# Three low parts taken from SBUF and one bank copied by ScalarE in the first gate/up unit

## The chip, the cores and the metric

The kernel runs on one core of a Trainium2 chip. The metric is the device time of one execution in microseconds (us), the median of the runs. The core has five engines with queues of their own: PE (TensorE, with its weight loads shown as PEld), DVE (VectorE), ACT (ScalarE), POOL (GpSimd) and SP, which here only issues transfers. Each engine takes its instructions in order, so an instruction that waits holds up everything behind it on that engine.

## The reference

One layer of a decoder on 512 tokens of width 2048, in float32: a combined input projection, two groups of attention heads, an output projection, a SwiGLU block and a last RMSNorm. The change touches the first matrix product of the SwiGLU block.

```python
D_MODEL = 2048; SEQ = 512
D_FF = -(-8 * D_MODEL // (3 * 256)) * 256          # 5632
...
x = x + mixed @ w_out[l]
h = rmsnorm(x, ln_ffn[l])
gate, up = jnp.split(h @ w_gate_up[l], 2, axis=-1)
x = x + (jax.nn.silu(gate) * up) @ w_down[l]
```

## The kernel before

**Rounded and low parts.** PE multiplies in a rounded float32 form (fp32r). To keep precision, every operand is split in two: a rounded part, "hi", which an ACT copy writes, and a low part, "lo" = value minus rounded part, which a DVE subtraction writes. Weights are stationary: tile `whi` holds their hi, `wlo` their lo (two buffers each). The other side lies in tiles whose 512 columns are 256 of hi and 256 of lo; a product takes `whi` against all 512 columns and `wlo` against the 256 of hi.

**Units and products.** `h @ w_gate_up` is done in 44 units (`Unit(j)`), each of 128 gate and 128 up columns. A unit cuts both sides into 2 by 2 blocks and makes seven block products in place of eight, in the order `PR` = 1, 7, 2, 5, 4, 6, 3. A product has a first half (four blocks of 128 rows, s = 0) and a second half (s = 1). In the first unit each half runs four matmuls with `whi` and then four with `wlo`. Products 1, 2 and 6 go to a PSUM bank named `m`, the others to one named `o`; product 6 is added onto the bank of product 1, 4 onto that of 7, 3 onto that of 5, so the earlier value is copied out first: `get_p1` and `get_p7` copy the banks of products 1 and 7 to slices of the SBUF tile `w4` (`w` in the profile).

**Weights of a product.** They are either loaded (`raw`, `rawx`) or a difference of loaded blocks that POOL makes (`sum`, tiles `t`; for products 7 and 5 of the first unit they share one tile, `t7`). `to_hp` lets ACT write a second rounded copy to a PSUM tile `hp`; `to_hi` lets ACT write the same values to `whi` in SBUF; `to_lo` lets DVE subtract `hp` from the weights. A `whi` buffer is free once the second half of the product two before has finished with it on PE.

**Other side.** It is made once and used by all 44 units. `form(p, s)` makes it for product p: "+" builds the sum or difference of blocks of `xh` (the scaled, transposed activations; `xh` again in the profile), "h" is the ACT copy and "l" the DVE subtraction. The tiles are named `hcs`, `hco`, `hca` and `hct`. The first halves (s = 0) and the second halves of products 1 and 7 are ready before the first unit; the second halves of 2, 5, 4, 6 and 3 are made while the first unit runs. Product 3's sum (`xh<-xh`) is POOL's, the others are DVE's.

**Order.** All of this stretch is in the order in which the code is written: `pV`, `pA`, `pG`, `pT` and `dma` record for DVE, ACT, POOL, PE and SP and keep that order (one helper, L118). `start_unit(n)` writes what follows product n of the first unit. Also there, on POOL, are five steps on tiles of 128x4 that make the scale of the second RMSNorm (`rv`, `rt`, `rq`), then a transfer (`q`), then product 3's sum.

**Buffers.** `e8` tiles (128 x 2048 floats) have three buffers in pool `side`: the tile `w4` of the first unit takes the buffer that `t7` had, so whatever writes `w4` first waits until every reader of `t7` is done; the last of these is the `to_lo` of product 5.

Of the kernel before, what the change touches and what calls it, by code (L numbers as in the profile page):

```python
# [12 lines left out]
AF = mybir.ActivationFunctionType  # L13
ALU = mybir.AluOpType
# [23 lines left out]
def tile_hymba(ctx: ExitStack, tc: tile.TileContext, x, ln_mix, w_in, sb_norm, swa_norm,  # L38
# [63 lines left out]
    def f(ap):  # L102
        return ap.bitcast(F32)
# [16 lines left out]
    pV, pA, pG, pT = Pinned(V), Pinned(A), Pinned(G), Pinned(nc.tensor)  # L120
# [792 lines left out]
    def h2_split(c, between=None):  # L913
        eV, eT = (pV, pT) if c == 3 else (V, nc.tensor)
        xh[c] = (o8.tile([P, 4, 512], F32, tag="o8", name="xh") if c < 2 else e8("xh"))
        if c == 3:
            two = zs[1].tile([P, 2, 512], F32, tag="hp", name="xt", bufs=2)
            pbs = [po(), po(), two[:, 0, :], two[:, 1, :]]
        else:
            pbs = [pz() for k4 in range(4)]  # L920
        for k4 in range(4):
            for t in range(NT):
                eT.transpose(out=pbs[k4][:, t * P:(t + 1) * P], in_=x2[c][:, t, k4 * P:(k4 + 1) * P], identity=ident)
        if between:
            between()
        for k4 in range(4):
            kt = c * 4 + k4
            eV.scalar_tensor_tensor(out=xh[c][:, k4, :], in0=pbs[k4], scalar=gcol[:, 16 + kt:17 + kt], in1=rs1["b"],
                                    op0=ALU.mult, op1=ALU.mult)
# [10 lines left out]
    def form(p, s, parts="+hl"):  # L940


        eV, eA = (pV, pA) if s and p not in "17" else (V, A)
        xa, xb = xh[2 * s], xh[2 * s + 1]
        a11, a21 = xa[:, :, 0:256], xa[:, :, 256:512]
        if p not in "17":
            a12, a22 = xb[:, :, 0:256], xb[:, :, 256:512]
        if "+" in parts:
            if p == "7":
                src = e8("s3")[:, 0:2, :].rearrange("p u (a b) -> p (u a) b", a=2)  # L950
                V.tensor_tensor(out=src, in0=a11, in1=a21, op=ALU.subtract)
            elif p == "5":
                src = a21
                eV.tensor_tensor(out=src, in0=a21, in1=a22, op=ALU.add)
            elif p == "6":
                src = a11
                eV.tensor_tensor(out=src, in0=a21, in1=a11, op=ALU.subtract)
            elif p == "3":
                src = a12
                (pG if s else G).tensor_tensor(out=src, in0=a12, in1=a11, op=ALU.subtract)  # L960
            else:
                src = {"1": lambda: a11, "2": lambda: a12, "4": lambda: a22}[p]()
            fsrc[p, s] = src
        src = fsrc[p, s]
        if "h" in parts:
            hc[p, s] = form_tile(p, s)
            eA.activation(out=hc[p, s][:, :, 0:256], in_=src, func=AF.Copy)
        if "l" in parts:
            hl = hc[p, s]
            eV.tensor_tensor(out=hl[:, :, 256:512], in0=src, in1=f(hl)[:, :, 0:256], op=ALU.subtract)  # L970
# [70 lines left out]
    def squares(c, ts):  # L1041
        for t in ts:
            pA.activation(out=junk, in_=x2[c][:, t, :], func=AF.Square, accum_out=ss2[:, t, c:c + 1])
# [4 lines left out]
    class Weights:  # L1048
# [15 lines left out]
        def to_lo(self, p):  # L1064
            src = self.src(p)
            self.lo[p] = wp.tile(list(src.shape), F32R, tag="wlo", name="wlo", bufs=2)
            pV.tensor_tensor(out=self.lo[p], in0=src, in1=f(self.hp[p]), op=ALU.subtract)

    class Unit(Weights):

# [73 lines left out]
            pA.activation(out=self.p1, in_=self.bank["1"], func=AF.Copy)  # L1144

        def get_p7(self):
            pV.tensor_copy(out=self.p7, in_=self.bank["7"])

        def get_c11(self):
            self.c = e8("c4")  # L1150
# [200 lines left out]
    def of(n, what):  # L1351

        if n < NP:
            getattr(units[n // 7], what)(PR[n % 7])
        elif n < NS:
            c, i = divmod(n - NP, 2)
            if what == "product":
                plain.product(c, i)
            elif i == 0:
                getattr(plain, what)(c)  # L1360
        elif n < NS + ND:
            getattr(passes[(n - NS) // 14], what)((PD[(n - NS) % 14 // 2], (n - NS) % 2))
# [30 lines left out]

    def between():
        squares(3, (3,))
        of(2, "to_hp")

    h2_split(3, between)
    units[0].product("1", ((1,),))
    upper.close()  # L1400
# [111 lines left out]
    def start_unit(n):  # L1512
        u = units[0]
        if n == 0:
            of(2, "to_hi")
            of(2, "to_lo")
            form("5", 1, "+")
            form("2", 1)
        elif n == 1:
            of(3, "to_hp")  # L1520
            of(3, "to_hi")
            of(3, "to_lo")
            u.get_w4()
            u.get_p7()
            form("5", 1, "hl")
        elif n == 2:
            of(4, "to_hp")
            of(4, "to_lo")
            form("4", 1)
            of(4, "to_hi")  # L1530
            u.get_p1()
        elif n == 3:
            form("6", 1, "+")
            of(5, "to_hp")
            of(5, "to_lo")
            of(5, "to_hi")
            form("6", 1, "hl")
            form("3", 1, "+")
        elif n == 4:
            of(6, "to_hp")  # L1540
            u.get_p75()
            of(6, "to_lo")
            form("3", 1, "hl")
            of(6, "to_hi")
        else:
            of(7, "to_hp")

    for n in range(NS + ND):
        if n > 1:
            run(n, "load")  # L1550
        run(n, "sum")
        if n > 5:
            of(n + 1, "to_hi")
            of(n + 1, "to_lo")
            of(n + 2, "to_hp")
        if n > 6:
            of(n, "product")
        elif n:
            units[0].product(PR[n], ((0,), (1,)))
        if n < 6:  # L1560
            start_unit(n)
        run(n, "take")
        run(n, "late")
# [95 lines left out]
```

## Time and profile before

| | |
|---|---|
| median of 3 runs | 2020.99 us (2020.88 to 2021.22) |
| profiled execution | 2021.5 us, of which its instructions span 2019.4 us |
| granted TensorE clock | 0.999 |
| PE busy | 2004.3 us, 99% of the span, 10412 matmuls |
| DVE, ACT busy | 1456.5 us, 1456.0 us (72% each) |
| POOL busy | 1030.2 us (51%) |
| the first unit's stretch | 722.7 to 746.2 us after the span's start |

In a row of the timeline, the columns are start in us from the span's start, duration in us, engine, line, operation, tile written <- tiles read, shape, count, and in brackets idle time of the engine just before it with what ended it. A duration runs to the end of the write; the next instruction of the engine can start some 0.1 us earlier, so steps on one engine are counted by the distance of their starts.

### The profile page before, as it was taken

What the parts mean: (1) busy time and instruction counts of PE and PEld (TensorE: products, weight loads), DVE (VectorE), ACT (ScalarE), POOL (GpSimd) and SP (SyncE); (2) the same over time, 40 slices, a digit from 0 to 9 for tenths busy, and PEclk for the clock granted to TensorE, in tenths of its full rate; (3) what the DMA queues carried; (4) which work ended last, traced back from release to release, by engine and by line L of the source; (5) the groups of instructions that cost most, each with busy time, mean ns of one, the idle gap of its engine ahead of it and who ended that gap; (6) DMA issues with size and microseconds to landing.
All of it is one profiled execution on the core that took longest, in us unless ns stands there. A gap on an engine that the chain in (4) does not pass through costs nothing. (4 is left out here: it accounts for less than half of the span.)

```text
span 2019.4 us, 29249 instructions
## 1 busy us (share of the span) xinstructions
PE 2004.3 (99%) x10412; PEld 1708.3 (85%) x10412; DVE 1456.5 (72%) x1968; ACT 1456.0 (72%) x2009; POOL 1030.2 (51%) x562
## 2 busy tenths in 40 slices
PE   9999999999999999999999999999999999999998
PEld 8888888898888888888888888888888888888886
DVE  4358888778963777777777777777777967767767
ACT  5347777657842478777777777777777688788787
POOL 0014444300100066766667666676666678878883
PEclk9999999999999999999999999999999999999999
DMA  5322222222343354453544535444354733533523
GB/s 188 94 84 73 63 63 73 64 77 71 105 146 115 117 160 121 115 141 100 136 116 120 138 100 139 113 123 133 103 141 109 288 130 107 178 132 105 175 86 115
DMA packets 286369, 240.23 MB, mean 119 GB/s; under 512 B 11024, under 2 KB 237392, under 8 KB 283792
## 3 DMA queue, kind: packets, MB, share of 16 engines
q1 hardware_dynamic: 285552, 235.71, 39.4%
q8 instruction: 82, 1.34, 0.3%
q0 software_dynamic: 288, 1.32, 0.2%
q10 hardware_dynamic: 384, 1.34, 0.2%
q14 instruction: 63, 0.52, 0.1%
HBM read 218.40 MB, written 19.92 MB: 118 GB/s over the span
## 5 line engine op out<-in xcount | busy, mean ns | idle before, releaser
L118 POOL TENSOR_TENSOR t<-raw,t 128x1024 f32<-128x1024 f32 x107 | 272.2, 2544 | 277.5 <-ACT hp L118 263.7
L118 DVE TENSOR_TENSOR wlo<-t,hp 128x1024 fp32r<-128x1024 f32 x235 | 286.4, 1219 | 172.3 <-PE o L118 108.1
L118 ACT ACTIVATE whi<-t 128x1024 fp32r<-128x1024 f32 x235 | 249.2, 1061 | 123.3 <-PE o L118 75.2
L118 PE MATMUL o<-hca,whi 128*128 128x512 f32 x880 | 307.5, 391 | 0.0
L118 POOL TENSOR_TENSOR t<-raw,raw 128x1024 f32<-128x1024 f32 x106 | 276.0, 2608 | 15.6 <-issue 10.9
L118 DVE TENSOR_TENSOR wlo<-raw,hp 128x1024 fp32r<-128x1024 f32 x175 | 213.5, 1220 | 79.9 <-issue 49.7
L118 ACT ACTIVATE whi<-raw 128x1024 fp32r<-128x1024 f32 (+1 forms) x177 | 187.1, 1057 | 99.9 <-PE m L118 72.1
L118 PE MATMUL o<-hca,wlo 128*128 128x256 f32 x880 | 244.0, 280 | 0.0
L118 ACT ACTIVATE hp<-t 128x1024 fp32r<-128x1024 f32 x235 | 237.0, 1008 | 0.3 <-DVE wlo L118 0.3
L220 DVE TENSOR_TENSOR wlo<-raw,whi 128x1024 fp32r<-128x1024 f32 x103 | 128.1, 1243 | 136.0 <-ACT whi L219 133.4
L219 ACT ACTIVATE whi<-raw 128x1024 fp32r<-128x1024 f32 x103 | 108.8, 1056 | 154.3 <-PE o L360 76.8
L118 PEld LDWEIGHTS o<-hca,whi 128*128 128x128 f32 x880 | 164.2, 187 | 35.8
L118 PE MATMUL m<-hca,whi 128*128 128x512 f32 x528 | 186.3, 392 | 1.1 <-DVE hca L118 1.1
L118 ACT ACTIVATE hp<-raw 128x1024 fp32r<-128x1024 f32 x179 | 180.7, 1010 | 3.2 <-DMA raw<-in_w_down_dram 2.3
L118 PEld LDWEIGHTS o<-hca,wlo 128*128 128x128 f32 x880 | 165.6, 189 | 0.4
L390 PE MATMUL m<-hhi,whi 128*128 128x512 f32 x384 | 156.3, 407 | 0.0
L391 PE MATMUL m<-hlo,whi 128*128 128x512 f32 x384 | 150.5, 392 | 0.0
L392 PE MATMUL m<-hhi,wlo 128*128 128x512 f32 x384 | 150.4, 392 | 0.0
L118 PE MATMUL o<-whi,dca 128*128 128x512 f32 x592 | 147.0, 389 | 1.5 <-DVE x2r L118 1.5
L118 PE MATMUL m<-whi,dca 128*128 128x512 f32 x592 | 146.9, 389 | 0.0
L118 PE MATMUL m<-hca,wlo 128*128 128x256 f32 x528 | 146.3, 280 | 0.0
L118 PEld LDWEIGHTS o<-whi,dca 128*128 128x128 f32 x592 | 111.1, 188 | 24.8 <-DVE x2r L118 1.9
(351 smaller groups left out, 5146.3 us busy)
## 6 DMA issues: line engine op xcount, KB each, us to landing
raw<-in_w_gate_up_dram SPq DMA_DIRECT2D x348, 256.0 KB, 5.2
raw<-in_w_down_dram SPq DMA_DIRECT2D x68, 512.0 KB, 4.9
raw<-in_w_in_dram SPq DMA_DIRECT2D x39, 512.0 KB, 3.6
raw<-in_w_in_dram SPq DMA_DIRECT2D x66, 256.0 KB, 3.3
raw<-in_w_out_dram SPq DMA_DIRECT2D x32, 512.0 KB, 3.9
aT<-w SPq DMA_DIRECT2D x44, 256.0 KB, 3.5
xd<-aT SPq DMA_DIRECT2D x10, 1024.0 KB, 7.1
rx<-in_w_down_dram SPq DMA_DIRECT2D x20, 512.0 KB, 5.1
```

Of the source, the lines that this page charges most:

```text
L118: return lambda *a, **k: tc.keep_in_program_order(fn(*a, **k))
L219: A.activation(out=hi, in_=raw, func=AF.Copy)
L220: V.tensor_tensor(out=lo, in0=raw, in1=f(hi), op=ALU.subtract)
L390: mm(o, lhsT=wh, rhs=xh, start=(k == 0), stop=False)
L391: mm(o, lhsT=wh, rhs=xl, start=False, stop=False)
L392: mm(o, lhsT=wl, rhs=xh, start=False, stop=(k == KT - 1))
```

## The change

The first unit's products 2, 5 and 4 no longer get the PSUM copy `hp`. Their low part is the weights minus `whi`, both in SBUF, so it waits for `to_hi`. For product 4 `to_hi` is moved ahead of `to_lo`. In the first unit the copy of product 7's bank to `w4` goes from DVE to ACT. All other units and products are as before.

```diff
         def to_lo(self, p):
...
-            pV.tensor_tensor(out=self.lo[p], in0=src, in1=f(self.hp[p]), op=ALU.subtract)
+            pV.tensor_tensor(out=self.lo[p], in0=src, in1=f(self.hp[p] if p in self.hp else self.hi[p]), op=ALU.subtract)
...
         def get_p7(self):
-            pV.tensor_copy(out=self.p7, in_=self.bank["7"])
+            if self.j:
+                pV.tensor_copy(out=self.p7, in_=self.bank["7"])
+            else:
+                pA.activation(out=self.p7, in_=self.bank["7"], func=AF.Copy)
...
     def between():
         squares(3, (3,))
-        of(2, "to_hp")
...
         elif n == 1:
-            of(3, "to_hp")
             of(3, "to_hi")
             of(3, "to_lo")
             u.get_w4()
             u.get_p7()
             form("5", 1, "hl")
         elif n == 2:
-            of(4, "to_hp")
+            of(4, "to_hi")
             of(4, "to_lo")
             form("4", 1)
-            of(4, "to_hi")
             u.get_p1()
```

ACT, from the last square of the attention output to the weights of product 4. The names are those above; `rawx` is product 2's weights in the first rows and product 4's in the last, `t` is product 5's, `hca` the second halves of products 2 and 5, `w` the copy of product 7's bank.

```order
 L118 ACTIVATE junk,ss_6209<-x_6068 128x512
-L118 ACTIVATE hp<-rawx 128x1024
 L118 ACTIVATE whi<-rawx 128x1024
 L118 ACTIVATE hca<-xh 128x4x256
-L118 ACTIVATE hp<-t_6883 128x1024
 L118 ACTIVATE whi<-t_6883 128x1024
+L118 ACTIVATE w_7005<-o 128x512
 L118 ACTIVATE hca<-xh 128x4x256
 L118 ACTIVATE rl<-rv 128x4
 L118 ACTIVATE rr<-rl 128x4
-L118 ACTIVATE hp<-rawx 128x1024
+L118 ACTIVATE whi<-rawx 128x1024
```

Three rounded copies are gone, the bank copy stands ahead of the rounded part of product 5's second half, and product 4's `whi` has come ahead of product 4's `hca`.

The same place on ACT in the changed kernel, with the engines that each instruction waits for.

```order
L118 ACTIVATE whi_6970<-rawx_6850 128x1024 [waits DMAHW7_49,DMAHW6_49,PE_49]
L118 ACTIVATE hca_6975<-xh_6933 128x4x256 [waits DVE_49]
L118 ACTIVATE whi_7001<-t7_6883 128x1024 [waits PE_49,Activation_49,Pool_49]
L118 ACTIVATE w4_7005<-o_6984 128x512 [waits DVE_49,Pool_49]
L118 ACTIVATE hca_7007<-xh_6759 128x4x256
L118 ACTIVATE rl_7010<-rv_6980 128x4 [waits Pool_49]
```

The bank copy waits for DVE and POOL: the counts in the built program are those of product 5's `to_lo` and of POOL's last read of `t7`. The `hca` behind it is product 5's.

DVE, at the same place.

```order
-L118 TENSOR_TENSOR wlo<-rawx,hp 128x1024
+L118 TENSOR_TENSOR wlo<-rawx,whi 128x1024
 L118 TENSOR_TENSOR xh<-xh 128x4x256
 L118 TENSOR_TENSOR hca<-xh,hca 128x4x256
 L118 TENSOR_REDUCE sst<-ss_6209 128x4
 L118 RECIPROCAL rq<-rstd_554 128x4
-L118 TENSOR_TENSOR wlo<-t_6883,hp 128x1024
-L118 COPY w_7009<-o 128x512
+L118 TENSOR_TENSOR wlo<-t_6883,whi 128x1024
 L118 TENSOR_TENSOR hca<-xh,hca 128x4x256
-L118 TENSOR_TENSOR wlo<-rawx,hp 128x1024
+L118 TENSOR_TENSOR wlo<-rawx,whi 128x1024
```

The order of DVE's work is the same without the bank copy; three subtractions read `whi` where they read `hp`. The rows of PE, POOL and SP are the same in both kernels.

## The prediction

> **What bounds the kernel now.** I read the page's busy line first, then who waited for whom on PE, then each engine's timeline in the first unit's stretch.
>
> ```profile
> PE 2004.3 (99%) x10412; PEld 1708.3 (85%) x10412; DVE 1456.5 (72%) x1968; ACT 1456.0 (72%) x2009; POOL 1030.2 (51%) x562
> PE o L118 <- DVE x2r L118: 1.5, 1, 1.5
> PE m L118 <- DVE hca L118: 1.1, 1, 1.1
> 722.70:746.20 23.50, 22.10 (x130) 19.08 (x129) 23.02 (x24) 20.91 (x27) 14.31 (x12) 1.00 0.49 153
> 746.20:765.70 19.50, 19.50 (x114) 17.07 (x113) 14.88 (x17) 16.75 (x19) 15.90 (x8) 1.00 0.34 96
> ```
>
> PE is busy 99% of the span: what delays it anywhere moves the end, and what doesn't costs nothing. Its longest waits are 1.5 us for `x2r`, which the change doesn't touch, and 1.1 us for an `hca`. The two last rows are windows: stretch, its length, then busy time of PE, PEld, DVE, ACT and POOL. In the first unit (722.7 to 746.2) DVE is busy 23.02 of 23.50 us; in the next unit 14.88 of 19.50, and PE doesn't wait. So in this one stretch DVE's queue paces the kernel. After it PE runs without a stall until `x2r`; a shift of PE here stays to the end.
>
> PE in that stretch (half products, `whi` part):
>
> ```profile
> 725.82 1.18 PE L118 MATMUL m<-hco,whi 128*128 128x512 f32 x4
> 731.51 1.08 PE L118 MATMUL m<-hca,whi 128*128 128x512 f32 x4
> 732.91 1.09 PE L118 MATMUL o<-hca,whi 128*128 128x512 f32 x4
> 734.33 1.21 PE L118 MATMUL o<-hca,whi 128*128 128x512 f32 x4
> 735.86 1.08 PE L118 MATMUL o<-hca,whi 128*128 128x512 f32 x4
> 741.32 1.20 PE L118 MATMUL m<-hca,whi 128*128 128x512 f32 x4 [1.11 <-DVE hca L118]
> 742.83 1.08 PE L118 MATMUL o<-hca,whi 128*128 128x512 f32 x4
> 744.67 1.20 PE L118 MATMUL o<-hct,whi 128*128 128x512 f32 x4 [0.30 <-DVE hct L118]
> 746.17 0.39 PE L118 MATMUL m<-hcs,whi 128*128 128x512 f32 x1
> ```
>
> A half product takes 1.40 us (731.51 to 732.91), and 0.13 more after a stall (734.33 to 735.86: 1.53). The rows at 731.51, 734.33, 741.32 and 744.67 are the second halves of products 2, 5, 6 and 3. From 735.86 to 741.32 are 5.46 us with three halves of 1.40 in them: about 1.3 us lost for product 6. From 742.83 to 744.67 are 1.84 us: 0.44 lost for product 3.
>
> ACT, DVE and POOL there:
>
> ```profile
> 727.04 1.06 ACT L118 ACTIVATE whi<-rawx 128x1024 fp32r<-128x1024 f32 x1 [1.15 <-PE m L118]
> 730.86 1.04 ACT L118 ACTIVATE hca<-xh 128x1024 fp32r<-128x1024 f32 x1
> 731.82 0.18 ACT L118 ACTIVATE rl<-rv 128x4 f32<-128x4 f32 x1
> 732.03 0.20 ACT L118 ACTIVATE rr<-rl 128x4 f32<-128x4 f32 x1
> 732.14 1.01 ACT L118 ACTIVATE hp<-rawx 128x1024 fp32r<-128x1024 f32 x1
> 735.11 0.60 ACT L118 ACTIVATE w<-m 128x512 f32<-128x512 f32 x1
> 735.60 1.02 ACT L118 ACTIVATE hp<-t 128x1024 fp32r<-128x1024 f32 x1
> 727.56 1.22 DVE L118 TENSOR_TENSOR wlo<-rawx,hp 128x1024 fp32r<-128x1024 f32 x1
> 728.70 1.22 DVE L118 TENSOR_TENSOR xh<-xh 128x1024 f32<-128x1024 f32 x1
> 729.83 1.22 DVE L118 TENSOR_TENSOR hca<-xh,hca 128x1024 fp32r<-128x1024 f32 x1
> 731.13 1.19 DVE L118 TENSOR_TENSOR wlo<-t,hp 128x1024 fp32r<-128x1024 f32 x1
> 732.46 0.69 DVE L118 COPY w<-o 128x512 f32<-128x512 f32 x1
> 733.06 1.22 DVE L118 TENSOR_TENSOR hca<-xh,hca 128x1024 fp32r<-128x1024 f32 x1
> 736.46 1.22 DVE L118 TENSOR_TENSOR xh<-xh 128x1024 f32<-128x1024 f32 x1
> 738.87 2.40 DVE L118 TENSOR_TENSOR hca<-xh,hca 128x1024 fp32r<-128x1024 f32 x1
> 742.92 1.70 DVE L118 TENSOR_TENSOR hct<-xh,hct 128x1024 fp32r<-128x1024 f32 x1
> 732.60 0.20 POOL L118 TENSOR_TENSOR rt<-rt,rv 128x4 f32<-128x4 f32 x1
> 733.17 1.17 POOL L118 TENSOR_TENSOR rt<-rt,rr 128x4 f32<-128x4 f32 x1
> 734.91 0.62 POOL L118 DMA_DIRECT2D q<-rq  x1 [0.29 <-POOL rq L118]
> 737.77 2.41 POOL L118 TENSOR_TENSOR xh<-xh 128x1024 f32<-128x1024 f32 x1 [2.24 <-DVE xh L118]
> 740.14 3.40 POOL L118 TENSOR_TENSOR t<-raw,raw 128x1024 f32<-128x1024 f32 x1
> ```
>
> The last rows show DVE and POOL blocking each other where DVE reads two SBUF tiles. Product 6's `hca` takes 2.40 us in place of 1.22 because POOL's `xh` runs until 740.18; POOL's `t` behind it takes 3.40 in place of 2.41; product 3's `hct` waits in turn until that `t` ends at 743.54. Even a 128x4 step (733.17) takes 1.17 us in place of 0.20: it ends at 734.34, just behind DVE's `hca` (733.06 to 734.28). Subtractions from `hp` don't take part.
>
> **The change, step by step.** Taken by itself it removes three ACT copies of about 0.95 us of ACT's queue, and 0.60 us from DVE (732.46 to 733.06); it adds one bank copy to ACT, 0.49 us of queue (735.11 to 735.60). The subtractions themselves cost the same.
>
> ```profile
> L118 DVE TENSOR_TENSOR wlo<-rawx,hp x2: 1216/1218/1220, 727.6 to 734.2; 128x1024 fp32r<-128x1024 f32 x2
> L970 DVE TENSOR_TENSOR hca<-xh,hca x4: 1212/1215/1217, 685.8 to 694.0; 128x1024 fp32r<-128x1024 f32 x4
> ```
>
> With one input in PSUM 1218 ns, with both in SBUF 1215. The Trainium skill, Perfetto Trace Analysis, section Optimizing Scalar/DVE Operations, gives DVE an access overhead of about 60 ns on SBUF against 125 on PSUM; by that the three would be an estimated 0.2 us shorter in all and the sum below 0.2 us smaller. These two rows don't show it, and I take nothing.
>
> Step 1, product 2. `wlo` now needs `whi`, which waits until PE has read product 1's `whi` (725.82 + 1.18 = 727.00): 727.04 to 728.10 as before. DVE's `wlo` starts at 728.13, not 727.56: 0.57 late, and all behind it in the queue. Product 2's `hca` ends at 729.83 + 1.22 + 0.57 = 731.62; PE wanted it at 731.51. Cost 0.16 + 0.13, about 0.3 us.
>
> Step 2, product 5. Its `wlo` starts at 731.13 + 0.57 = 731.70 and ends at 732.90. ACT's bank copy writes `w4`, in the buffer of `t7`, which this `wlo` reads: it starts at 732.93. Queued behind it is product 5's `hca` on ACT: 732.93 + 0.49 = 733.42, to 734.46, where before it began at 730.86. DVE waits for it from 732.84, so the 0.60 saved there is lost again: `hca` on DVE 734.49 to 735.71, before 733.06 to 734.28. PE starts that half at 735.76, not 734.33: 1.43 us late, step 1 included.
>
> Step 3, up to product 6. Behind `hca` ACT takes `rl` (0.96 later), `rr` (0.21) and product 4's `whi` (0.11): 734.70 to 735.75. DVE's queue follows at its distance of 1.14 (727.56 to 728.70): `wlo` 735.78, `hca` 736.92, `xh` 738.06 to 739.28, before 736.46 to 737.68. Product 6's `hca` needs that `xh` through one ACT copy (739.31 to 740.35), so DVE could start it at 740.38. Product 4 itself is in time: PE wants its second half at 735.76 + 1.53 + 1.40 = 738.69, and its `hca` ends near 738.2.
>
> Step 4, the port. POOL's five small steps now meet four DVE instructions in a row that read two SBUF tiles each (`hca`, `wlo`, `hca`, `xh`), with no `hp` or bank copy between. After `rr` (734.59 to 734.79) POOL's first step comes at 734.9 and gets its turn when the DVE instruction on hand lets go, and so on: about 735.8, 737.0, 738.2, 739.4, the fifth at 739.6. That POOL does get a turn between two such instructions, at little cost to DVE, these rows show:
>
> ```profile
> 168.96 0.43 DVE L629 TENSOR_TENSOR l<-e,h 128x256 fp32r<-128x256 f32 x1
> 169.31 0.77 DVE L675 TENSOR_TENSOR l<-e,h 128x512 fp32r<-128x512 f32 x1
> 169.06 0.49 POOL L646 COPY af<-e 128x128 f32<-128x128 f32 x1
> ```
>
> The transfer `q` follows 0.3 later and takes 0.62, so POOL's `xh` comes at about 740.6: after DVE has begun product 6's `hca` at 740.38. That one then runs undisturbed to 741.60 (PE wants it at 735.76 + 1.53 + 3 x 1.40 = 741.49), but POOL's `xh` runs from 741.5 to 743.9, its `t` from there to 746.3; ACT's copy for `hct` ends at 745.04, DVE's `hct` waits for `t` and ends at 747.35. PE begins product 3's second half at 747.4, not 744.67: 2.7 us late. If POOL came first instead, `xh`, `hca`, `t` and `hct` would still stand one after another on the same port from 740.4 on, and end at the same 747.4.
>
> Nothing behind it makes this longer: POOL's later sums are as late as PE is. Transfers start when buffers come free, so they shift too.
>
> Sum: 0.3 (step 1) brought to 1.43 by step 2 and to 2.7 by step 4, which takes in the stalls that were there. The profiled execution took 2021.5 us (span 2019.4); a like one would take 2024.2 (span 2022.1). The median of the runs, 2020.99, is 0.5 lower: 2023.7 us. That is 0.13% more, within the 0.2% that a measurement of this kernel can tell from no change.
>
> Bounds: all stalls of the stretch gone would be 23.50 - 22.10 = 1.4 us, with the restarts about 2.2, the least time 2018.8. The most is one more turn of the port, below.
>
> **Rivals.**
>
> A: the small POOL steps aren't held, or once only, as before (one of five). Then POOL's `xh` starts behind DVE's at 739.3 and ends at 741.7; product 6's `hca` ends at 742.87, `t` at 745.2, `hct` at 746.3. PE 746.35: 1.7 us late, 2022.7. For it speaks that only one of five was held before, against it that those met the bank copy and `hp`. The Trainium skill, SBUF — State Buffer, section Who interferes with whom, says that the one that comes first keeps the port for its whole instruction and the other blocks fully, whatever the size. That is on the side of step 4, as is the row at 733.17.
>
> B: the bank copy doesn't hold ACT, so that the change does what it says. DVE would be 0.57 later by step 1 and 0.74 sooner without its copy (732.32 to 733.06), 0.2 us sooner at product 6, and the time 2020.8. Against it: ACT takes its rows in order, and the copy's wait is in the program.
>
> C, slower: product 3's `hct` loses one more turn, to POOL's next `t`. That costs a further 2.4 us (737.77's length): 5.1 us late, 2026.1. It decides whether ACT's copy for `hct` ends (745.04) before POOL's first `t` does (746.3): 1.3 us in hand.
>
> **How the numbers follow.** My forecast, 2023.1 to 2024.3, has 0.55; A 0.22; B, and any gain, 0.10; C 0.06; 0.07 is left for something between forecast and C. The range from 2021.8 to 2024.8 holds forecast and A with their margins; it leaves out B and C. Over 2025.0 lie C and a little more: slower 0.07. Under 2017.0 lies nothing I can name: faster 0.01.
>
> **What would show it.** In the changed profile: DVE's `wlo<-rawx,whi` near 728.1; ACT's `w<-o` near 732.9, right behind `wlo<-t,whi`; DVE idle about 1.6 us before product 5's `hca`, waiting for ACT; PE stalled before product 5's second half by over 1 us; `rt` steps of about 1.2 us on POOL; `hca` of product 6 near 1.2 us and `hct` long; the next unit's first matmul near 748.9 in place of 746.17. The forecast is wrong if the bank copy starts before 732, if the `rt` steps take 0.2 us, or if PE waits somewhere later for something that was in time before.

## The result, and the profile after

The changed kernel takes 2026.54 us (median of 7 runs, 2025.12 to 2028.27), the kernel before 2020.60 (7 runs, 2018.71 to 2021.22). The ratio is 1.0031, with a 95% interval from 1.0022 to 1.0040: slower by 0.3%, some 6 us. The forecast was 2023.7, its range up to 2024.8.

The profiled execution took 2026.16 us (span 2024.1, granted clock 0.997). PE's rows in its timeline, for the halves shown of before:

```profile
722.68 1.10 PE L118 MATMUL m<-hcs,whi 128*128 128x512 f32 x4
735.79 1.19 PE L118 MATMUL o<-hca,whi 128*128 128x512 f32 x4 [1.11 <-DVE hca L118]
746.44 2.07 PE L118 MATMUL m<-hca,whi 128*128 128x512 f32 x4 [4.81 <-DVE hca L118]
749.17 1.85 PE L118 MATMUL o<-hca,whi 128*128 128x512 f32 x4
751.33 1.09 PE L118 MATMUL o<-hct,whi 128*128 128x512 f32 x4
752.73 0.39 PE L118 MATMUL m<-hcs,whi 128*128 128x512 f32 x1
```

Against before, product 5's second half begins 1.46 us later (735.79, 734.33), product 6's 5.12 (746.44, 741.32), product 3's 6.66 (751.33, 744.67). From the first unit's first matmul to the next unit's it takes 30.05 us (722.68 to 752.73). Before, from 722.74 to 746.17, it took 23.43. This length serves as the measure of every experiment.

The spans differ by 4.7 us only, not by these 6.6: the profiled execution of before had the 1.5 us wait for `x2r` behind the units, and that of the changed kernel did not; at that place its lag behind before falls from 6.6 to 4.8 us. The wait is there in ten of the 17 profiled executions of this document, and each kernel has one profile only. That it comes and goes between executions of the same kernel is inferred: the seven timed runs of before spread from 2018.71 to 2021.22. So medians are compared below only beside the lengths.

ACT, DVE and POOL (DVE's last row runs beside the two POOL rows above it):

```profile
732.93 0.60 ACT L118 ACTIVATE w<-o 128x512 f32<-128x512 f32 x1 [2.02 <-POOL rv L118]
733.42 1.05 ACT L118 ACTIVATE hca<-xh 128x1024 fp32r<-128x1024 f32 x1
734.51 1.23 DVE L118 TENSOR_TENSOR hca<-xh,hca 128x1024 fp32r<-128x1024 f32 x1 [1.67 <-ACT hca L118]
734.89 0.91 POOL L118 TENSOR_TENSOR rt<-rr 128x4 f32<-128x4 f32 x1 [2.00 <-ACT rr L118]
739.97 0.62 POOL L118 DMA_DIRECT2D q<-rq  x1 [0.29 <-POOL rq L118]
740.62 2.39 POOL L118 TENSOR_TENSOR xh<-xh 128x1024 f32<-128x1024 f32 x1
742.95 2.35 POOL L118 TENSOR_TENSOR t<-raw,raw 128x1024 f32<-128x1024 f32 x1
740.52 5.86 DVE L118 TENSOR_TENSOR hca<-xh,hca 128x1024 fp32r<-128x1024 f32 x1
```

Up to 740.6 all is as forecast. Then DVE's `hca` of product 6, ready at 740.52 (0.10 us ahead of POOL's `xh`), takes 5.86 us. POOL's `xh` and, right behind it, `t` take their undisturbed 2.39 and 2.35 us, and `hca` ends at 746.38, 1.08 us behind `t`. Before, where it lost one turn at the port, `hca` ended 1.09 us behind `xh` (741.27, 740.18); here it ended that far behind the next POOL instruction, so it lost two turns. In the traces of before and after, dozens of other DVE instructions with two SBUF inputs are lengthened beside POOL; none of them loses more than one turn.

The windows show the second thing. Columns are stretch, its length, busy time of PE, PEld, DVE, ACT and POOL, then the granted clock, DMA share and GB/s:

```profile
740.58:743.99 3.41, 1.05 (x7) 0.77 (x5) 3.41 (x1) 1.78 (x2) 3.38 (x3) 1.00 0.20 29
743.99:747.40 3.41, 0.96 (x2) 0.83 (x3) 3.41 (x3) 2.01 (x3) 2.24 (x2) 0.50 1.03 278
747.40:750.82 3.42, 3.42 (x11) 2.83 (x10) 3.42 (x4) 2.27 (x4) 3.34 (x2) 0.50 0.38 108
750.82:754.23 3.41, 3.41 (x22) 3.02 (x21) 3.28 (x5) 1.99 (x3) 1.88 (x2) 1.00 0.97 257
```

While PE stood idle, its clock fell to half at 743.99 and stayed there until 750.82. So the halves from 746.44 and 749.17 take 2.73 and 2.16 us to the next, not 1.53 and 1.40: 1.96 us more.

### The profile page after: what moved, and what is told of

Same layout as the page of the kernel before. It is cut to its first block, busy times and chain, and to the rows that moved or that the text cites. A ratio compares the mean times of both kernels' runs of the same rounds, so it can differ in the third digit from the quotient of the medians.

```text
span 2024.1 us, 29247 instructions
## 1 busy us (share of the span) xinstructions
PE 2005.8 (99%) x10412; PEld 1709.6 (84%) x10412; DVE 1456.3 (72%) x1967; ACT 1453.9 (72%) x2007; POOL 1032.4 (51%) x562
## 4 chain that ended last, share of the span: by engine, by line
PE 97%; DVE 2%; ACT 1%; issue 0%; POOL 0%; DVEq 0%; ACTq 0%; POOLq 0%
PE o L118 34%; PE m L118 28%; PE m L390 4%; PE m L391 4%; PE m L392 4%; PE m L359 2%; PE m L358 2%; PE m L360 2%; PE o L360 2%; PE o L359 2%; PE o L358 2%; PE z L118 1%; PE z L359 1%; PE z L360 1%; PE z L358 1%; PE o L685 1%
```

## The experiments

Length is from the first unit's first matmul to the next unit's, in the profiled execution; medians and ratios are of the timed runs, each ratio against runs of before on the same chip, whose medians lay between 2019.7 and 2021.0 (it is estimated from all runs, not the quotient of two medians). The last three ran once, with a profile.

| run | length | median (runs) | ratio to before, 95% interval |
|---|---|---|---|
| before | 23.43 | 2020.60 (7) | |
| changed | 30.05 | 2026.54 (7) | 1.0031, 1.0022 to 1.0040 |
| copy_only | 24.57 | 2022.26 (10) | 1.0008, 0.9998 to 1.0017 |
| hp_only | 28.17 | 2024.64 (10) | 1.0021, 1.0012 to 1.0031 |
| copy_behind | 24.23 | 2021.63 (10) | 1.0007, 0.9998 to 1.0016 |
| copy_behind_hp | 23.61 | 2021.30 (10) | 1.0005, 0.9995 to 1.0015 |
| filled | 28.97 | 2025.31 (7) | 1.0027, 1.0016 to 1.0038 |
| pool_later | 27.59 | 2023.45 (10) | 1.0017, 1.0008 to 1.0027 |
| dve_later | 29.88 | 2026.99 (5) | 1.0034, 1.0021 to 1.0047 |
| dve_later2 | 29.60 | 2026.97 (5) | 1.0034, 1.0020 to 1.0048 |
| t_behind | 27.32 | 2024.31 (10) | 1.0018, 1.0008 to 1.0027 |
| before_tie | 25.09 | 2020.79 (10) | 1.0005, 0.9995 to 1.0014 |
| q_behind | 25.36 | 2022.23 (10) | 1.0007, 0.9998 to 1.0016 |
| before_q | 27.37 | 2025.16 (10) | 1.0022, 1.0012 to 1.0032 |
| q_memset | 28.92 | 2024.95 (1) | |
| q_memset2 | 31.32 | 2028.75 (1) | |
| memset_mid | 26.33 | 2022.40 (1) | |

**The parts of the change.** copy_only is the kernel before with the bank copy on ACT; hp_only is the changed kernel with that copy back on DVE, so only the three `hp` are gone.

```diff
 copy_only, against before:
-            pV.tensor_copy(out=self.p7, in_=self.bank["7"])
+            if self.j:
+                pV.tensor_copy(out=self.p7, in_=self.bank["7"])
+            else:
+                pA.activation(out=self.p7, in_=self.bank["7"], func=AF.Copy)
 hp_only, against the changed kernel: the same lines the other way
```

> The kernel before, with only the bank copy of product 7 moved from DVE to ACT (hp kept for products 2, 5 and 4). Theory: wlo of product 5 ends at 732.3, the copy starts then, hca of product 5 ends on DVE at 735.1 (734.3 before); product 4's whi ends at 737.0 and holds PE; POOL's small steps meet subtractions from hp and run free; POOL's xh at 738.7, hca of product 6 asks at 740.5, loses one turn, ends at 742.2; next unit's first matmul 747.2, 1.0 us over before (within the scatter of the runs). If the copy's wait alone were the whole loss: next unit near 752, 6 us over before.

> The changed kernel, with the bank copy back on DVE: only the low parts of products 2, 5 and 4 are taken from SBUF. Theory: hca of product 5 ends at 734.8 (734.3 before), POOL's small steps are each held by DVE, POOL's xh comes near 739.3 and DVE's hca of product 6 near 739.4: within about 0.1 us again. If POOL is clearly first, hca loses one turn and ends at 742.8, next unit's first matmul 747.7, 1.5 us over before; if it is a tie that costs two turns, hca ends near 745.1, the clock drops, and the next unit comes at 750 to 751.5, 4 to 5 us over before. If the low parts cost nothing: next unit 746.2, as before.

The copy alone cost 1.14 us, PE waiting 0.83 for product 5's `hca`. Without the `hp`, 4.74 were lost. There four of POOL's small steps are held, `rq` the last, and DVE lost two turns:

```profile
736.57 1.06 POOL L118 TENSOR_TENSOR rq<-rq,rt 128x4 f32<-128x4 f32 x1
737.92 0.62 POOL L118 DMA_DIRECT2D q<-rq  x1 [0.29 <-POOL rq L118]
738.57 2.39 POOL L118 TENSOR_TENSOR xh<-xh 128x1024 f32<-128x1024 f32 x1
738.76 5.59 DVE L118 TENSOR_TENSOR hca<-xh,hca 128x1024 fp32r<-128x1024 f32 x1
```

So of the two parts, each tried alone, the removed PSUM copies bring the larger loss. The next run shows that they need not.

In copy_behind the bank copy stands behind product 5's `hca` on ACT, so that it holds up only what comes later; copy_behind_hp does the same with the three `hp` kept.

```diff
-            u.get_w4()
-            u.get_p7()
             form("5", 1, "hl")
+            u.get_w4()
+            u.get_p7()
```

> The changed kernel, with the bank copy on ACT moved behind product 5's second half (hca), so that hca no longer queues behind the wait for wlo. Theory (step 2 of the forecast, then the port): hca of product 5 ends at 734.0 and PE isn't stalled there; product 4's weights come later on ACT behind the copy, xh of product 6 ends at 738.3, POOL's xh starts with it, hca of product 6 loses one turn and ends at 741.8; next unit's first matmul at 746.8, 0.6 us over before. Rival (the wait of the copy doesn't matter, the SBUF low parts alone bring the loss): next unit at 749 or later, 3 us or more over before.

> The kernel before, with the bank copy of product 7 on ACT and behind product 5's second half, hp kept. Theory: DVE's queue is 0.7 us shorter and nothing waits for the copy; xh of product 6 ends at 737.0, POOL's xh runs to 739.5, hca of product 6 loses one turn and ends at 740.6 (741.3 before), hct at 744.0; next unit's first matmul at 745.6, 0.6 us under before. If DVE's queue doesn't pace the stretch: 746.2, as before.

In copy_behind product 5 has no stall, and the small steps are over before DVE's run of port instructions, `q` at 736.04 to 736.66. POOL's `xh` waits 1.39 us for DVE's `xh`, and DVE's `hca` loses one turn (2.38 us):

```profile
734.35 0.20 POOL L118 TENSOR_TENSOR rt<-rt,rr 128x4 f32<-128x4 f32 x1
738.05 2.40 POOL L118 TENSOR_TENSOR xh<-xh 128x1024 f32<-128x1024 f32 x1 [1.39 <-DVE xh L118]
739.14 2.38 DVE L118 TENSOR_TENSOR hca<-xh,hca 128x1024 fp32r<-128x1024 f32 x1
```

The length is 24.23: of the change's 6.62 us, 5.8 go with the place of one ACT copy. This doesn't contradict hp_only. With `hp` gone the loss appears where POOL's small steps run into DVE's run of port instructions; in copy_behind they come while DVE stands idle (0.93 us up to 734.46), and only one of the five is held. With `hp` kept it is 23.61. A gain of 0.6 was expected there and 0.2 was lost: product 4's `whi`, now behind the bank copy on ACT, keeps PE waiting for 0.41 us. Neither of the two beats the kernel before, nor does any other run.

**The clock.** In filled PE is kept at work: 14 matmuls with weights of zero are added to product 6's bank between its halves.

```diff
+    zero = ft("zero", [P, P], F32R)
+    pG.memset(f(zero), 0.0)
...
+                if self.j == 0 and p == "6" and sl == (1,):
+                    for _ in range(14):
+                        pT.matmul(b, lhsT=zero, rhs=hc[p, 0][:, 0, :], start=False, stop=False, skip_group_check=True)
```

> The changed kernel, with 14 matmuls with all-zero weights added onto product 6's bank between its halves, where PE otherwise idles 4.8 us: they take about 3.2 us. Clock theory (the halves after the stall took 2.7 and 2.2 us in place of 1.5 and 1.4 because the granted clock fell to 0.5 during the stall): clock 1.0 throughout, hca still 5.9 us, product 6's second half again at 746.4 and then at full speed; product 3's second half waits for hct (749.9), next unit's first matmul at 751.5 in place of 752.7; time 5.2 us over before, 1.2 under the changed kernel. Rival (the slow halves come from transfers or the port, not from idling): same stamps as the changed kernel, next unit at 752.7.

DVE lost its two turns again (5.95 us), but the clock stayed whole (PE's timeline, then a window):

```profile
741.60 3.36 PE L118 MATMUL m<-hca,zero 128*128 128x512 f32 x14
746.63 0.73 PE L118 MATMUL m<-hca,whi 128*128 128x512 f32 x2 [1.67 <-DVE hca L118]
```

```profile
746.40:748.30 1.90, 1.67 (x9) 1.50 (x10) 1.90 (x4) 1.41 (x2) 1.58 (x1) 1.00 0.56 134
```

The length fell by 1.08 us, to 28.97. The two slow halves cost 1.96, but at full speed PE then waits 0.56 for `hct`, so part of the slow clock lies over that wait.

**Who comes first at the port.** In pool_later a memset of an unused tile delays POOL's `xh`, so that DVE asks first: the branch of the forecast. In dve_later DVE's product-5 sum comes ahead of `hca`, so that POOL asks first by a clear margin. The theory at that time was that the second turn is lost in a tie, when both ask within a few tenths of a microsecond.

```diff
 pool_later:
             form("6", 1, "hl")
+            pG.memset(junk, 0.0)
             form("3", 1, "+")
 dve_later (and the same line removed after product 4):
+            u.get_p75()
             form("6", 1, "hl")
```

> The changed kernel, with a memset of a spare SBUF tile (0.3 to 0.6 us) on POOL ahead of product 3's sum xh, so that DVE asks some 0.4 us before POOL. Tie theory: DVE's hca of product 6 runs undisturbed, about 1.22 us, to 741.8; POOL's xh follows to 744.1 and its t to 746.5; hct ends at 747.6; PE stalls 2.9 us before product 3's second half, and the clock may drop there: next unit's first matmul 749.2 to 751.1, time 3.0 to 4.9 us over before. Rival (POOL's pair keeps the port): hca again above 4 us, next unit near 753.

> The changed kernel, with DVE's update of the copied bank (w<-o,w, 0.6 us, one input in PSUM) moved ahead of the low part of product 6's second half. DVE then asks for that hca near 741.0 us, when POOL's xh has been running since 740.6. Tie theory (the two turns were lost because DVE and POOL asked within 0.1 us of each other): hca loses one turn only and takes about 3.1 us, to 744.1; hct ends near 747.5; the next unit's first matmul (746.17 before, 752.73 in the changed kernel) comes at 749.0, or up to 751 if the TensorE clock still drops; time 2.8 to 4.8 us over before. Rival (POOL keeps the port whenever two of its instructions stand back to back): hca ends at 746.4 again, next unit near 752.7, 6.4 us over before.

pool_later:

```profile
740.24 1.23 DVE L118 TENSOR_TENSOR hca<-xh,hca 128x1024 fp32r<-128x1024 f32 x1
740.80 2.91 POOL L118 TENSOR_TENSOR xh<-xh 128x1024 f32<-128x1024 f32 x1
745.80 1.19 PE L118 MATMUL o<-hca,whi 128*128 128x512 f32 x4 [2.61 <-ACT whi L118]
747.43 1.91 PE L118 MATMUL o<-hct,whi 128*128 128x512 f32 x4
```

`hca` ran undisturbed, as the forecast had it, yet 4.16 us were lost, not 2.7. PE stalled at product 3's first half: its `whi` stands behind `hct` on ACT, and `hct` needs POOL's `xh`, which ends at 743.71. The clock fell as well, for 3.4 us from 747.14: the last half took 2.56 us (747.43 to the next unit at 749.99), not 1.50, and the half before it 1.63, not 1.53. In dve_later DVE asked 0.38 us after POOL's `xh` had begun, and `hca` still took 5.39 us.

**How near, and what stands behind.** dve_later2 adds a copy of 0.68 us to DVE ahead of `hca`; t_behind makes POOL's `t` wait for `hca`; before_tie brings the two requests together in the kernel before.

```diff
 dve_later2, against dve_later:
             u.get_p75()
+            pV.tensor_copy(out=junk, in_=u.bank["5"])
 t_behind, against the changed kernel:
             form("3", 1, "+")
+            pG.tensor_copy(out=junk[:, 0:4], in_=f(hc["6", 1])[:, 0, 256:260])
 before_tie, against before:
             form("6", 1, "hl")
+            pG.tensor_copy(out=junk[:, 0:4], in_=xh[2][:, 0, 0:4])
+            pG.memset(junk, 0.0)
             form("3", 1, "+")
```

> The changed kernel with DVE's product-5 sum (0.68 us) moved ahead of product 6's hca, and a copy of the same bank into an unused tile (about 0.6 us) behind it, so that DVE asks for the port about 1.0 us after POOL's xh has begun (740.2), not 0.1 before (changed kernel) or 0.38 after (the run dve_later). Theory (DVE loses a second turn only where it asks within about 0.4 us of the first POOL sum's start): hca begins near 741.2, takes about 2.5 us and ends 1.1 us behind POOL's xh, near 743.7; POOL's t takes 3.4 us instead of 2.35; PE waits about 2.3 us, its clock falls for a short while or not at all; the next unit begins between 748.5 and 750; time 2022.5 to 2024.5. Rival (what counts is that another POOL sum stands right behind xh and that DVE is late): hca ends near 746 again, PE waits 4.7 us, the next unit near 752, time near 2027.

> The changed kernel with one 128x4 copy on POOL between its xh and its t that reads product 6's hca, so that t can't stand right behind xh but waits until DVE has that hca. DVE and POOL ask for the port as in the changed kernel (740.5 and 740.6). Theory (the second lost turn goes to the POOL sum right behind): DVE waits for xh alone, hca ends 1.1 us behind it, near 744.1 (3.6 us long, not 5.86); POOL's t begins near 744.5; PE waits 2.5 us; hct, one turn lost to t, near 748; the next unit at 749.5 with full clock, up to 750.5 if the clock falls; time 2023 to 2024.5. Rival (the 5.86 us have another cause than the port, such as a late read or write of hca's tile): hca 5 us or more, the copy and t behind it, the next unit at 752 or later.

> The kernel before, nothing of the change in it, with two POOL instructions ahead of its xh for product 3: a 128x4 copy that reads product 6's sum (so that it can't run early) and a 128x512 memset of an unused tile. POOL's xh then begins near 738.5 to 738.7 instead of 737.77; DVE asks for product 6's hca at 738.87 as before. Theory (it is the nearness of the two requests, not the change, that costs the second turn): hca takes 5 to 5.7 us and ends near 744.3, PE waits 4 us at product 6 and its clock falls to 0.5 for 3 to 7 us; the next unit 3.5 to 5.5 us late, at 749.7 to 751.7; time 2023 to 2026. Rival (DVE loses one turn as everywhere else in this kernel): hca ends 1.1 us behind xh, near 742.1, PE waits 1.9 us, the next unit at 747.2, time 0.9 us above the kernel before.

dve_later2, then t_behind, then before_tie:

```profile
739.92 2.38 POOL L118 TENSOR_TENSOR xh<-xh 128x1024 f32<-128x1024 f32 x1
742.25 2.35 POOL L118 TENSOR_TENSOR t<-raw,raw 128x1024 f32<-128x1024 f32 x1
740.89 4.80 DVE L118 TENSOR_TENSOR hca<-xh,hca 128x1024 fp32r<-128x1024 f32 x1
```

```profile
740.69 2.38 POOL L118 TENSOR_TENSOR xh<-xh 128x1024 f32<-128x1024 f32 x1
744.23 0.19 POOL L118 CAST junk<-hca 128x4 bf16<-128x4 f32 x1 [1.16 <-DVE hca L118]
740.60 3.56 DVE L118 TENSOR_TENSOR hca<-xh,hca 128x1024 fp32r<-128x1024 f32 x1
```

```profile
737.64 2.38 POOL L118 TENSOR_TENSOR xh<-xh 128x1024 f32<-128x1024 f32 x1
739.99 3.38 POOL L118 TENSOR_TENSOR t<-raw,raw 128x1024 f32<-128x1024 f32 x1
738.03 3.08 DVE L118 TENSOR_TENSOR hca<-xh,hca 128x1024 fp32r<-128x1024 f32 x1
```

The tie theory fell from both sides: asked 0.97 us behind POOL, two turns lost; asked 0.39 behind, one. That the second loss goes to the sum right behind `xh` held: in t_behind `hca` ends 1.09 us behind `xh` (744.16, 743.07).

**The transfer.** In every run so far with two turns POOL's `xh` had followed its transfer `q` at once (739.97 + 0.62, then 740.62). In every run with one it had not, but for t_behind, where `t` couldn't stand right behind `xh`: in copy_behind `xh` began 1.39 us behind `q`. q_behind moves `q` behind `t`; before_q puts it ahead of `xh` in the kernel before.

```diff
 q_behind, against the changed kernel:
-    (2, rstd2_make), (2, rstd2_out), (7, rstd2_bc)
+    (2, rstd2_make), (5, rstd2_out), (7, rstd2_bc)
 before_q, against before (rstd2_out taken from the list above):
             form("6", 1, "hl")
+            pG.tensor_copy(out=junk[:, 0:4], in_=xh[2][:, 0, 0:4])
+            rstd2_out()
             form("3", 1, "+")
```

> The changed kernel with POOL's transfer q moved behind its t, so that POOL's xh follows the last small step (rq) and not the transfer; xh then begins near 739.8 and DVE asks for product 6's hca at 740.5 as before. New theory (DVE loses the second turn where POOL's xh follows its transfer q at once; how far apart the two ask does not count): one turn lost, hca 2.7 us, ending near 743.2, 1.1 us behind POOL's xh; POOL's t 3.4 us; PE waits 1.7 us at product 6 and keeps its full clock; hct about 746.6; the next unit 25.4 us (25 to 26.5) after the first unit's start, time 2022 to 2023.5. Rival (the change's order on DVE costs the second turn, whatever POOL did ahead): hca 5 us or more, t 2.35 us, the next unit 29 us or more after the first unit's start, time 2025.5 or more.

> The kernel before, nothing of the change in it, with POOL's transfer q moved from 734.9 to directly ahead of its xh for product 3 (and a 128x4 copy of product 6's sum ahead of q, so that it can't run early): the run before_tie with the transfer in place of the memset. New theory (xh right behind the transfer costs DVE the second turn): hca 5.3 to 5.9 us long, POOL's t 2.35 us right behind xh, PE waits 4 us at product 6 and its clock falls to 0.5, the next unit 27.5 to 30 us after the first unit's start (23.43 before), time 2023.5 to 2027. Rival (one turn, as in before_tie): hca 3 to 3.5 us, t 3.4 us, 25 to 25.5 us, time 2021 to 2022.5.

q_behind, then before_q:

```profile
739.69 2.40 POOL L118 TENSOR_TENSOR xh<-xh 128x1024 f32<-128x1024 f32 x1
742.05 3.39 POOL L118 TENSOR_TENSOR t<-raw,raw 128x1024 f32<-128x1024 f32 x1
745.38 0.62 POOL L118 DMA_DIRECT2D q<-rq  x1
740.59 2.58 DVE L118 TENSOR_TENSOR hca<-xh,hca 128x1024 fp32r<-128x1024 f32 x1
```

```profile
737.69 0.62 POOL L118 DMA_DIRECT2D q<-rq  x1
738.34 2.39 POOL L118 TENSOR_TENSOR xh<-xh 128x1024 f32<-128x1024 f32 x1
740.67 2.36 POOL L118 TENSOR_TENSOR t<-raw,raw 128x1024 f32<-128x1024 f32 x1
738.58 5.54 DVE L118 TENSOR_TENSOR hca<-xh,hca 128x1024 fp32r<-128x1024 f32 x1
```

Both came as expected, but for before_q's length, 0.13 us under its range. With everything of the change in it and `q` out of the way the length is 25.36, one turn lost, the clock whole (expected 25.4). With nothing of the change but `q` there it is 27.37, against 25.09 in before_tie, which has a memset at that place; its ratio, 1.0022, is close to hp_only's 1.0021. Timing does not separate the two kinds of run: DVE asked 0.90 us behind POOL in q_behind and lost one turn, 0.97 behind in dve_later2 and lost two.

How close it must be: q_memset puts a memset between `q` and `xh`, memset_mid one between `xh` and `t`.

```diff
 q_memset, against dve_later2; q_memset2 the same with DVE's extra copy into a row of w4 that nothing uses:
             form("6", 1, "hl")
+            pG.memset(junk, 0.0)
             form("3", 1, "+")
 memset_mid, against the changed kernel:
             form("3", 1, "+")
+            pG.memset(junk, 0.0)
```

> The run dve_later2 with a 128x512 memset between POOL's transfer q and its xh, so that xh begins 0.55 us later, near 740.4, and still 0.4 to 0.5 us ahead of DVE's hca. If only an xh directly behind the transfer costs the second turn: hca 3.0 to 3.2 us, POOL's t 3.4 us. If the transfer still works in the background and anything within a microsecond counts: hca 5.2 to 5.5 us, POOL's t 2.35 us.

In q_memset the memset and DVE's extra copy write the same tile, so the memset waited for the copy and DVE came first: `hca` took 1.21 us, and the run says nothing on the question.

> The run q_memset again, with DVE's extra copy into another unused tile than POOL's memset, so that the memset doesn't wait for that copy: transfer q, memset, xh, t on POOL, with xh near 741.0 and DVE's hca asked 0.4 to 0.6 us after it. If only an xh directly behind the transfer costs the second turn: hca 3.0 to 3.2 us, POOL's t 3.4 us. If a transfer half a microsecond back still counts: hca 5.2 to 5.5 us, POOL's t 2.35 us.

> The changed kernel with a 128x512 memset between POOL's xh and its t, which waits for nothing. If POOL keeps the port over every instruction that stands ready behind xh: hca ends 1.1 us behind t, 6.4 us long. If DVE only loses to one further instruction: hca ends about 1.1 us behind the memset, 4.1 us long; if it wins against a memset, 3.6 us.

q_memset2, then memset_mid:

```profile
739.48 0.62 POOL L118 DMA_DIRECT2D q<-rq  x1 [0.29 <-POOL rq L118]
740.10 0.55 POOL L118 MEMSET junk<- 128x512 bf16 x1
740.59 2.36 POOL L118 TENSOR_TENSOR xh<-xh 128x1024 f32<-128x1024 f32 x1
741.10 5.25 DVE L118 TENSOR_TENSOR hca<-xh,hca 128x1024 fp32r<-128x1024 f32 x1
```

```profile
739.98 2.39 POOL L118 TENSOR_TENSOR xh<-xh 128x1024 f32<-128x1024 f32 x1
742.28 0.55 POOL L118 MEMSET junk<- 128x512 bf16 x1
739.89 3.57 DVE L118 TENSOR_TENSOR hca<-xh,hca 128x1024 fp32r<-128x1024 f32 x1
```

A transfer 0.49 us back still costs the second turn (5.25 us); between that and the 1.39 us of copy_behind nothing was tried. Each of these readings rests on one profile per kernel. A memset behind `xh` lets DVE in: `hca` ends at 743.46, 1.09 us behind `xh`, through the memset. The Trainium skill, SBUF — State Buffer, section Who interferes with whom, says that a DVE instruction with two SBUF inputs contends with POOL instructions that read SBUF and not with those that only write it; this run agrees.

## Why the prediction was wrong

Step 1 held: `wlo` of product 2 at 728.07 (forecast 728.13). So did step 2, to a few hundredths: bank copy 732.93, `hca` on ACT 733.42, DVE idle for 1.67 us, PE at 735.79 (forecast 735.76). Step 3 held: product 6's `hca` could start at 740.52 (forecast 740.38), and product 4 was in time. Of step 4 the first half held: four small steps of 0.91 to 1.25 us on POOL, `xh` at 740.62 (forecast 740.6). Rivals A and B fell with that.

What failed is step 4's end, first in who comes first: the forecast had DVE's `hca` start 0.2 us ahead of POOL's `xh` and run undisturbed. By the stamps it was 0.10 us ahead, and POOL ran first. For that case step 4 said: "If POOL came first instead, `xh`, `hca`, `t` and `hct` would still stand one after another on the same port … and end at the same 747.4". The order was `xh`, `t`, `hca`, `hct`. That put product 6's `hca` 4.8 us behind its place (746.38, forecast 741.60), and the stall fell on product 6's second half instead of on product 3's: two halves that should have run ahead of the stall now stood behind it. Where the order was as assumed, in q_behind, PE began product 3's second half at 746.57 and 1.93 us were lost over before (forecast 747.4 and 2.7; POOL came 0.9 us sooner there, without `q`). The cause of the other order is shown, as far as it goes, by before_q and q_behind: `q` shortly ahead of two POOL sums in a row. Both parts of the change put it there. `q` moved by 5.06 us, from 734.91 to 739.97: POOL's first `rt` step began 2.57 later (734.89, before 732.32), because `rr` stood on ACT behind the waiting bank copy and product 5's `hca`, and four held steps in place of one added 2.49. Why a transfer does this is not settled: no view shows who holds the port.

Second, the sum had no term for the clock. The claim "Nothing behind it makes this longer" was wrong: two halves took 1.96 us more, worth 1.08 net (filled). So of the 6.62 us lost, 2.7 are the forecast's, some 2.8 more go with the other order at the port (filled, with the clock whole, lost 5.54), and 1.08 with the clock.

Third, the other branch, DVE first and undisturbed, was mis-sized too: in pool_later it cost 4.16 us and not 2.7. Of the 1.46 more, 1.16 are the clock again (1.06 in the last half, 0.10 in the one before). For the rest, step 4 left out that product 3's `whi` stands behind `hct` on ACT: it held the half before until 745.80, so that at full clock the last half could have begun at 747.33, while its own `hct` ended at 747.12.

Rival C, the slower one, had nearly the right size (2026.1) for the wrong place: `hct` lost one turn only (1.89 us at 748.04); it was `hca` that lost two.

## What to carry to other kernels

A shared port has to be read as a queue with its order, not as a sum of durations: ask which of the waiting instructions the next matmul needs, and what the sum is if another comes first. When small steps of an engine are held, look at what they push ahead of the next large one; here a transfer of 0.62 us had moved by 5 us to a bad place, and with it out of the way (q_behind) 4.7 of the 6.6 us were gone. A stall of PE of more than some 1.7 us within one step of the clock's grid (below) carries a second price, the clock, which filler matmuls can take away (filled).

## What the runs showed of the hardware

The clock's marks lie on a grid that goes on through the whole run. In the changed kernel the granted clock first rose 6.71 us after the span's start and fell at 743.99, 737.28 us later, which is 216 times 3.4133; it rose at 750.82, two steps on. By the runs below, what counts is how busy PE is within one step, and where the steps lie differs from run to run. In before_tie a wait of 1.79 us lay in one step and halved the clock; in memset_mid 2.50 us fell on two steps and did not (windows of before_tie, then of memset_mid; the clock is the third column from the end):

```profile
738.61:742.02 3.41, 1.62 (x10) 1.25 (x9) 3.41 (x3) 2.27 (x3) 3.41 (x2) 1.00 0.80 223
742.02:745.43 3.41, 3.41 (x13) 2.92 (x12) 3.41 (x4) 3.41 (x5) 3.41 (x2) 0.50 0.66 188
```

```profile
738.83:742.24 3.41, 2.19 (x14) 1.76 (x12) 3.35 (x2) 1.94 (x2) 3.08 (x3) 1.00 0.05 5
742.24:745.65 3.41, 2.14 (x11) 1.88 (x12) 3.41 (x4) 2.01 (x2) 3.41 (x3) 1.00 0.88 232
```

In copy_behind a step with 1.76 us busy kept its clock, and in dve_later2 one with 1.68 (739.27 to 742.68). So the limit lies near half of a step; one step of hp_only, with 1.51 us busy by its stamps, did not lower the clock, while one of dve_later with 1.46 did. That would fit the others only if the steps are read some 0.2 us earlier than they are stamped, which no view shows. The Trainium skill, TensorE: Matmul & The Clock Gate, section Part 1: The HAM clock gate, gives a free-running window of 3413 ns, which agrees, and half clock after an idle window; here a window half idle was enough.

Of the ports that DVE and POOL share, the Trainium skill, SBUF — State Buffer, section Who interferes with whom, says that they are an exclusive lock and that issue order decides who blocks. For the first turn the runs agree where the two starts lie 0.19 us or more apart (hp_only is the nearest). Where DVE's stamp is 0.09 or 0.10 us ahead (changed, filled, t_behind, memset_mid), POOL ran first, so there the stamps don't show the order of issue, or it does not decide. The section doesn't say who is next: here DVE, waiting since 740.52, lost to a POOL instruction that began at 742.95, and in these runs that happened only with a POOL transfer shortly ahead.
